# Chunk states kept by group and chunk instead of by chunk and group, in a two-layer S5 and attention network

## The chip, the core and the metric

One core of one Trainium2 chip runs the whole program. The engines are PE (the matmul engine; PEld is its weight load, which runs beside the matmuls), VectorE (DVE in the profile), ScalarE (ACT), POOL and SP, which issues the DMAs. The metric is the device time of one execution in microseconds; before the change it is 2419.13 us, the median of three runs (2417.30 to 2419.89).

## What is computed

The reference is a two-layer network for 128 prompt tokens and 512 sample tokens of 1024 features. Each layer normalizes and modulates its input, projects it, and runs three branches beside each other: a bidirectional state space scan (S5), a window attention and a global attention. They are merged with gates, projected, and followed by an MLP. What matters here is the S5 branch: 32 groups of 16 channels, 64 complex states per group and direction.

```python
def _s5_bidirectional(u, lam_re, ..., s0):
    lam_bar = jnp.exp(lam * step)
    b_bar = ((lam_bar - 1.0) / lam)[..., None] * lax.complex(b_re, b_im)
    for d, rev in ((0, False), (1, True)):
        bu = jnp.einsum('blgc,gpc->blgp', uf, b_bar[d])
        if s0 is not None:                      # the sample has an initial state
            bu = bu.at[:, n_tok - 1 if rev else 0].add(lam_bar[d] * s0c)
        _, states = lax.associative_scan(_ssm_combine, (a, bu), reverse=rev, axis=1)
        y = y + jnp.einsum('blgp,gcp->blgc', states, c_mat[d]).real
        finals.append(states[:, 0] if rev else states[:, -1])
```

The outputs are the two token arrays, the prompt's final S5 states and its keys and values.

## The kernel before

The tokens are cut into chunks of 8. There are 84 chunk columns: 16 of the prompt, 64 of the sample, and 4 of padding. The states at the chunks' starts are kept in one tile per layer, `st`, on 128 partitions (64 states of the forward direction, 64 of the backward one), and along a partition in the order [chunk, real/imaginary, group], 84 x 2 x 32 floats. It is made, changed and used in this order, once per layer:

- `s5_in` (L588), once for each four groups: 8 matmuls of 84 columns (L596), then ScalarE copies the forward half into `st` one column later (L598) and VectorE the backward half, turned round within prompt and sample (L600).
- `s5_states` (L633): POOL clears the padding, then the scan over the chunks runs in pairs of columns. `pairs(2, 3)` (L654) adds lambda^8 times each even column to the next one, in four pieces, three on VectorE and one on POOL, each of two multiplies (L660) and two adds (L661). SP copies the sample's initial state into column 19 (L664). Then come 31 dependent steps on POOL (L677 to L680), four instructions each, which carry the state two columns on; the first 8 do prompt and sample together (128 elements), the rest the sample (64 elements). `pairs(1, 2)` fills in the columns between. ScalarE takes the prompt's final state (L684), and ScalarE and VectorE turn the backward columns round again (L689 to L691).
- The outputs of the chunks (L1010 to L1026): for each group one matmul with the chunk's own inputs (L1023, moving operand `ub`) and two with the states (L1025, moving operand `st[:, :, r_, g_]`, which steps over the chunks). Each matmul of this type (float32) leaves two records in the trace.

Around this run the other branches: the key and query projections, evicted by VectorE and ScalarE (L717 to L719, L782 to L785), the window attention (L855 to L977), the low parts of the weights (L124, whose high parts come from L123) and gates worked out ahead (L813). L792 on POOL raises the queries' sums of squares to a power. The code of the two layers is the same; in layer 1 `s5_states` comes before the key projections, in layer 0 behind them. Each engine takes its instructions in one fixed order, which a scheduler has chosen with its own cost model from the program text and its dependences, so a change in one place can reorder the instructions around it on all engines.

Elsewhere, the tile `yT` is kept as [feature block, token in the chunk, chunk] and is read and written with the token in the chunk as the inner index (`y_views`, L1057), which is a step of 84 floats. Its instructions are L120 to L124 by way of `split_y` (L1062), and L1133.

Of the kernel before, what the change touches and what calls it, by code (L numbers as in the profile page):

```python
# [15 lines left out]
NT = 5                      # token tiles of 128: 0 the prompt, 1..4 the sample  # L16
D = 1024
NCH = 84                    # chunk columns: [pad, 16 prompt, pad, pad, 64 sample, pad]
# [5 lines left out]
AHEAD = ((0, 1, 4, 2, 4, 1), (1, 0, 1, 2, 4, 1))   # gates worked out ahead: beside the queries, the scan, beside its outputs, around the GLU, by layer  # L24
# [3 lines left out]
SPLITS = ((0, 3), (3, 5))   # token-tile ranges of a feature-major product  # L28


def net(tc, I, O, depth=DEPTH, dbg=None):
# [37 lines left out]
    # ---------------------------------------------------------------- constants  # L69
# [38 lines left out]
    # persistent work  # L108
# [8 lines left out]
    def split(hi, lo, src, half=False):  # L117
        """src (or src / 2) as a high part and the exact rest"""
        if half:
            S.activation(hi, src, AF.Copy, scale=0.5)  # L120
            V.scalar_tensor_tensor(lo, src, 0.5, hi, op0=ALU.mult, op1=ALU.subtract)
        else:
            S.activation(hi, src, AF.Copy)  # L123
            V.tensor_tensor(lo, src, hi, op=ALU.subtract)  # L124

    def wtile(src, K, slot=None):
        """a packed weight tile [128, 1024] of K row blocks as its high and low parts: [(hi, lo)] by row block"""
# [17 lines left out]
    def tok(a, t0, t1):  # L145
        """the token tiles t0..t1 of a view [128, NT, 128], or of the views of the two parts of SPLITS"""
# [5 lines left out]
    def mm_fm(out, ws, acts, t0, t1, ks=None, first=True, last=True):  # L152
        """feature-major: out [128 f, tokens] += w[k].T @ act[k]; ws[k] = (hi, lo) [128, 128];
        acts[k] = (hi, lo) views of the tokens"""
# [8 lines left out]
    def mm_tm(out, ws, acts, t, first=True, last=True):  # L163
        """token-major: out [128 tok, n] += act[k][:, t].T @ w[k]; ws[k] = (hi, lo) [128, n]"""
# [9 lines left out]
    # ---------------------------------------------------------------- adaLN modulation  # L174
    def mods_steps(l, rounds, tmp, tmp2=None, acc=False):
        """the modulation vectors of a layer, 2048 columns a round, one row block of the weight a step"""
        if rounds[0] == 0:
            SY.dma_start(bmodT, I["bmodT"][:, l])
        for r in rounds:
# [22 lines left out]
            # the gates as rows  # L202
# [11 lines left out]
    def affine(l, w):  # L214
        """affA/affB[l][:, w]: h = xhat * A + B; w 0: before w_in, 1: before w_up"""
# [11 lines left out]
    # ---------------------------------------------------------------- h: transposed, modulated, split  # L227
    def new_h():
        """high and low parts, each in the two parts of SPLITS"""
# [26 lines left out]
    # ---------------------------------------------------------------- layer norm of a token tile  # L256
    def ln_stat(st):
        """mean, rstd, - mean rstd from the bn_stats of the chunks"""
# [8 lines left out]
    def ln_tile(z, st):  # L267
        """z [128, 1024] -> (z - mean) * rstd in place; st: bn_stats of its chunks"""
# [4 lines left out]
    # ---------------------------------------------------------------- S5 tables (weights only)  # L273
    def s5_prep(l, pp, after=None, use=None):
# [25 lines left out]
        def poly(o, r, cs):  # L300
            """cs: from the highest power, to the constant"""
# [8 lines left out]
        def expm1(o, x, plus1=False):  # L310
            """exp(x) - 1 (or exp(x)): x = k ln2 + r"""
# [8 lines left out]
            tt(q, q, r, ALU.add)                       # e^r - 1  # L320
# [3 lines left out]
            p2 = ti.bitcast(F32)                       # 2^k  # L324
# [12 lines left out]
        # sin and cos - 1 of th: th = q 2pi + r, a = r/4, two doublings  # L337
# [19 lines left out]
        # powers of lam_bar: Pw[:, ri, k, g], k = 0..8; n = lam_bar - 1  # L357
# [27 lines left out]
        # b_bar = (lam_bar - 1) / lam * b  # L385
# [13 lines left out]
        # ec[t]: fwd lam^(t+1), bwd lam^(8-t);  ei[j]: fwd lam^(7-j), bwd lam^j  # L399
# [12 lines left out]
        for b in range(8):  # L412
# [31 lines left out]
            # C lam^e and its negated imaginary part  # L444
# [10 lines left out]
            # lag kernel of these four groups; stationary columns: [full | fwd | bwd]  # L455
# [15 lines left out]
            # input operator, built with states on partitions and transposed  # L471
# [20 lines left out]
    # ---------------------------------------------------------------- phase A  # L492
    def phase_a(l, h):
# [9 lines left out]
        if l == 0:  # L503
# [3 lines left out]
            # the rows of a partial sum over four row blocks: one from each strip  # L507
# [4 lines left out]
            # the first three row blocks of the S5 input go along  # L512
# [3 lines left out]
            def mods0(g_):  # L516
                """shift and scale of 256 features"""
# [57 lines left out]
        # entry states by chunk column, the backward direction turned round inside each segment  # L575
        st = sp.tile([128, NCH, 2, 32], F32, name="st")
# [11 lines left out]
        def s5_in(b, io):  # L588
            """what the chunks of four groups add to the states"""
# [15 lines left out]
        # ---- S5 input, to the chunked layout  # L605
# [27 lines left out]
        def s5_states():  # L633
            """the states at the chunks' starts"""
# [6 lines left out]
            # ---- scan over chunks: entry[i + 1] = lam^8 entry[i] + v, prompt and sample side by side, in pairs:  # L641
            # w = lam^8 v[i] + v[i + 1]; entry[i + 2] = lam^16 entry[i] + w one after the other; the entries between them
# [11 lines left out]
            def pairs(src, dst):  # L654
                """dst + 2 k += lam^8 (src + 2 k), all 41 pairs of columns"""
# [8 lines left out]
            SY.dma_start(st[:, 19], I["state0"][:, l])  # L664
# [17 lines left out]
            # final states of the prompt  # L682
# [691 lines left out]
    h = None  # L1374
# [3 lines left out]
    for p in (wp, ps, dram, base):  # L1378
        p.release()


# ---- host: layouts only
def pack(inp):
    import numpy as np

# [88 lines left out]
```

## Time and profile before

| what | value |
|---|---|
| median of three runs | 2419.13 us (2417.30 to 2419.89) |
| the profiled execution, first to last instruction | 2422.9 us |
| busy: PE, PEld, DVE, ACT, POOL | 2305.5, 2201.2, 1501.1, 992.3, 567.6 us |
| chain that ended last, by engine | PE 78%, DVE 8%, POOL 6%, DMA 3%, ACT 2%, issue 2% |
| mean granted clock of PE | 0.977 of full speed |
| scan of layer 0 and of layer 1 on POOL | about 216 to 282 us, and 1360 to 1430 us |

Only the span of the profiled execution is recorded for it, so it also stands for its own time; it is 3.8 us above the median of the runs. Matmuls are pipelined, so the distance between two starts tells what one costs, and the length of one contains the waiting of the pipeline. A window of the span shows which engine is full in a stage; the waits show who stood for whom; the groups by line and shape give the duration of one instruction.

### The profile page before, as it was taken

How to read it: one execution, taken by the hardware profiler on the slowest of the kernel's cores; microseconds unless marked ns; L12 is line 12 of the kernel's file. 1: busy time of each engine (PE TensorE's matmuls, PEld its weight loads, DVE VectorE, ACT ScalarE, POOL GpSimd, SP SyncE). 2: the span in 40 equal slices, each digit the busy share in tenths (PEclk: the TensorE clock that was granted, in tenths of full speed). 3: DMA queues.
4: the chain of work that ended last, by engine and by line, in shares of the span. 5: the costliest groups of instructions: out<-in, count | busy, mean ns of one | idle time of the engine just before them, and what ended most of it. 6: DMA issues, size and time to landing. Idle time of an engine off the chain costs nothing.

```text
span 2422.9 us, 43760 instructions
## 1 busy us (share of the span) xinstructions
PE 2305.5 (95%) x17304; PEld 2201.2 (91%) x17304; DVE 1501.1 (62%) x3091; ACT 992.3 (41%) x2320; POOL 567.6 (23%) x665
## 2 busy tenths in 40 slices
PE   7887999999999999999999889999999889999997
PEld 4777897799999999999999889999999889999997
DVE  6887854766357966654664766466744873444467
ACT  2324655574344333222234256467643343232221
POOL 2555700001024211100541651000102350000056
PEclk8998999999999999999999999999999999999999
DMA  7423236612241344455326223511222332222221
GB/s 261 144 82 103 97 111 225 230 68 89 72 158 54 115 164 157 162 174 200 122 97 189 72 67 111 158 61 71 77 75 72 146 100 75 76 73 79 71 73 59
DMA packets 126381, 278.25 MB, mean 115 GB/s; under 512 B 40640, under 2 KB 60224, under 8 KB 126176
## 3 DMA queue, kind: packets, MB, share of 16 engines
q1 hardware_dynamic: 126176, 275.45, 33.5%
q8 instruction: 136, 2.23, 0.4%
q14 instruction: 69, 0.57, 0.1%
HBM read 240.97 MB, written 38.63 MB: 115 GB/s over the span
## 4 chain that ended last, share of the span: by engine, by line
PE 78%; DVE 8%; POOL 6%; DMA 3%; ACT 2%; issue 2%; SPq 0%; DVEq 0%; ACTq 0%; POOLq 0%
PE p_g L159 9%; PE p_g L161 9%; PE p_g L160 9%; PE p_sc L170 4%; PE p_sc L172 4%; PE p_sc L171 4%; PE p_g L170 4%; PE p_sc L160 4%; PE p_g L171 4%; PE p_sc L161 4%; PE p_sc L159 4%; PE p_g L172 4%; PE p_pt L947 2%; PE p_g L1025 2%; POOL sa L677 1%
## 5 line engine op out<-in xcount | busy, mean ns | idle before, releaser
L124 DVE TENSOR_TENSOR wlo<-raw,whi 128x512 fp32r<-128x512 f32 x472 | 364.5, 785 | 194.4 <-ACT whi L123 188.6
L123 ACT ACTIVATE whi<-raw 128x512 fp32r<-128x512 f32 x472 | 293.5, 630 | 416.8 <-PE p_sc L172 138.8
L159 PE MATMUL p_g<-hh,whi 128*128 128x384 f32 (+1 forms) x1200 | 379.4, 316 | 2.8 <-ACT mt L802 2.6
L161 PE MATMUL p_g<-hh,wlo 128*128 128x384 f32 (+1 forms) x1200 | 377.4, 315 | 2.5 <-DVE wlo L124 2.2
L160 PE MATMUL p_g<-hl,whi 128*128 128x384 f32 (+1 forms) x1200 | 377.8, 315 | 0.0
L159 PEld LDWEIGHTS p_g<-hh,whi 128*128 128x128 f32 x1200 | 227.8, 190 | 10.1 <-ACT rl L1274 5.8
L161 PEld LDWEIGHTS p_g<-hh,wlo 128*128 128x128 f32 x1200 | 227.7, 190 | 4.3 <-DVE wlo L124 3.7
L160 PEld LDWEIGHTS p_g<-hl,whi 128*128 128x128 f32 x1200 | 228.2, 190 | 0.6 <-issue 0.5
L159 PE MATMUL p_sc<-hh,whi 128*128 128x256 f32 (+1 forms) x672 | 209.1, 312 | 9.1 <-ACT hh L123 8.8
L160 PE MATMUL p_sc<-hl,whi 128*128 128x256 f32 (+1 forms) x672 | 208.2, 310 | 4.1 <-DVE hl L124 4.1
L161 PE MATMUL p_sc<-hh,wlo 128*128 128x256 f32 (+1 forms) x672 | 208.4, 310 | 1.5 <-DVE wlo L124 1.5
L1090 POOL TENSOR_TENSOR mt<-sg,mt 128x640 f32<-128x640 f32 x24 | 41.2, 1719 | 652.1 <-DVE stat L934 272.4
L170 PE MATMUL p_sc<-whi,ff 128*128 128x256 f32 x680 | 192.9, 284 | 0.0
L172 PE MATMUL p_sc<-whi,ff 128*128 128x256 f32 x680 | 192.3, 283 | 0.0
L171 PE MATMUL p_sc<-wlo,ff 128*128 128x256 f32 x680 | 191.1, 281 | 0.0
L170 PE MATMUL p_g<-whi,hh 128*128 128x256 f32 x544 | 161.8, 299 | 10.8 <-DVE rt L785 6.6
L171 PE MATMUL p_g<-wlo,hh 128*128 128x256 f32 x544 | 161.3, 297 | 8.9 <-DVE wlo L124 8.6
L172 PE MATMUL p_g<-whi,hl 128*128 128x256 f32 x544 | 159.8, 295 | 0.0
L124 DVE TENSOR_TENSOR pl<-p_pt,ph 128x512 fp32r<-128x512 f32 (+1 forms) x176 | 102.8, 589 | 69.0 <-ACT ph L123 60.8
L159 PEld LDWEIGHTS p_sc<-hh,whi 128*128 128x128 f32 x672 | 131.0, 195 | 15.3 <-ACT hh L123 9.7
L159 PE MATMUL p_g<-act,whi 128*128 128x384 f32 x448 | 140.3, 313 | 3.7 <-ACT mtmp L192 2.3
L170 PE MATMUL p_g<-whi,ff 128*128 128x256 f32 x500 | 142.0, 284 | 0.0
(410 smaller groups left out, 6371.8 us busy)
## 6 DMA issues: line engine op xcount, KB each, us to landing
raw<-in_w_mod_dram SPq DMA_DIRECT2D x96, 512.0 KB
raw<-in_w_up_dram SPq DMA_DIRECT2D x64, 512.0 KB
raw<-in_w_down_dram SPq DMA_DIRECT2D x64, 512.0 KB
raw<-in_w_gate_dram SPq DMA_DIRECT2D x48, 512.0 KB
raw<-in_w_br_dram SPq DMA_DIRECT2D x24, 512.0 KB
raw<-in_w_q_dram SPq DMA_DIRECT2D x16, 512.0 KB
ctab_d<-prow SPq DMA_DIRECT2D x16, 512.0 KB
tab<-ctab_d SPq DMA_DIRECT2D x16, 512.0 KB
```

The lines of the kernel that those rows point to most:

```text
L123: S.activation(hi, src, AF.Copy)
L124: V.tensor_tensor(lo, src, hi, op=ALU.subtract)
L159: T.matmul(out, wh, tok(ah, t0, t1), start=(first and k == 0), stop=False)
L160: T.matmul(out, wh, tok(al, t0, t1), start=False, stop=False)
L161: T.matmul(out, wl, tok(ah, t0, t1), start=False, stop=(last and k == n - 1))
L170: T.matmul(out, ah, wh, start=(first and k == 0), stop=False)
L171: T.matmul(out, ah, wl, start=False, stop=False)
L172: T.matmul(out, al, wh, start=False, stop=(last and k == n - 1))
L677: G.tensor_tensor(a[:, 0:ns], at(cur), lb(M[:, 0]), op=ALU.mult)
L947: T.transpose(p[:, (2 * (z - z0) + z_) * 128:(2 * (z - z0) + z_ + 1) * 128], Ps[z_][:, z * 128:(z + 1) * 128], ident)
L1025: T.matmul(o, ct[:, r_, q], st[:, :, r_, g_], start=False, stop=(r_ == 1))
L1090: G.tensor_tensor(mtv[:, ft], sg, mtv[:, ft], op=ALU.add)
```

## The change

`st` becomes a view of a tile `stm` whose order along a partition is [real/imaginary, group, chunk]. All instructions of the scan keep their code, their element order and their number, and address the new tile through the view. The matmuls of the chunk outputs read the tile directly. The initial state is copied by DMA into a small tile `s0` of its own, and from there by VectorE into column 19. The final state's copy is written for the new order. The rest of the difference takes away comments.

```diff
-        # entry states by chunk column, the backward direction turned round inside each segment
-        st = sp.tile([128, NCH, 2, 32], F32, name="st")
+
+        stm = sp.tile([128, 2, 32, NCH], F32, name="st")
+        st = stm.rearrange("p r g c -> p c r g")
         segs = ((0, 18), (18, 84))
...
             pairs(2, 3)
-            SY.dma_start(st[:, 19], I["state0"][:, l])
+            s0 = sp.tile([128, 2, 32], F32, name="s0")
+            SY.dma_start(s0, I["state0"][:, l])
+            V.tensor_copy(st[:, 19], s0)
...
-            S.activation(fin, st[:, 17].rearrange("p a b -> p (a b)"), AF.Copy)
-            # the backward direction back into chunk order
+            S.activation(fin.rearrange("p (a b) -> p a b", a=2), st[:, 17], AF.Copy)
+
...
-                    T.matmul(o, ct[:, r_, q], st[:, :, r_, g_], start=False, stop=(r_ == 1))
+                    T.matmul(o, ct[:, r_, q], stm[:, r_, g_], start=False, stop=(r_ == 1))
```

In the rows of order below, the changed kernel's line numbers are one higher from L577 on and three higher from L667 on (L660 and L661 are L661 and L662 there, L684 is L687, L792 is L795).

VectorE, layer 0, the start of `pairs(2, 3)`, before the change. `VV` and `KL` belong to the attention's keys, `kf` are keys, `ub` is the product's buffer:

```order
L124 TENSOR_TENSOR VV<-vf_1506,VV 128x10x64
L660 TENSOR_TENSOR ub<-st,lam_100 128x640
L124 TENSOR_TENSOR KL<-p_pt,KH 128x512
L752 TENSOR_TENSOR kf_2012<-kf_2012,ksq 128x640
L124 TENSOR_TENSOR KL<-p_pt,KH 128x512
L661 TENSOR_TENSOR st<-st,ub 128x10x64
```

The same place in the changed kernel:

```order
L124 TENSOR_TENSOR VV<-vf_1506,VV 128x10x64
L661 TENSOR_TENSOR ub<-st,lam_100 128x640
L755 TENSOR_TENSOR kf_2012<-kf_2012,ksq 128x640
L124 TENSOR_TENSOR KL<-p_pt,KH 128x512 x2
L662 TENSOR_TENSOR st<-st,ub 128x10x64
```

The pairs keep their place, but for the order of their neighbours.

POOL, layer 0, the end of the scan, before:

```order
L678 TENSOR_TENSOR sb<-st,l_2176 128x64
L679 TENSOR_TENSOR sa<-sa,st 128x64
L680 TENSOR_TENSOR st<-sa,sb 128x64
L792 TENSOR_TENSOR ssq<-ssq,mh 128x40
L1090 TENSOR_TENSOR mt<-sg,mt 128x640 x8
```

And in the changed kernel, with three whole steps still to come:

```order
L681 TENSOR_TENSOR sb<-st,l_2176 128x64
L682 TENSOR_TENSOR sa<-sa,st 128x64
L795 TENSOR_TENSOR ssq<-ssq,mh 128x40
L683 TENSOR_TENSOR st<-sa,sb 128x64
L680 TENSOR_TENSOR sa<-st,l_2176 128x64
```

The power of the queries' sums has moved from behind the scan to between two instructions of its 28th step of 31.

ScalarE, layer 0, behind the scan, before. `fin` is the final state, the first instruction that waits for the scan's end; `whi`, `ph`, `P` and `gt` belong to weights, attention and gates:

```order
L123 ACTIVATE ph<-p_pt 128x512
L123 ACTIVATE ph<-p_pt 128x256
L684 ACTIVATE fin<-st 128x64
L689 ACTIVATE ub<-st 64x576
L938 ACTIVATE P,stat<-p_sc,stat 128x512 x2
L813 ACTIVATE gt<-p_g 128x384
L691 ACTIVATE st<-ub 64x576
```

And in the changed kernel:

```order
L941 ACTIVATE P,stat<-p_sc,stat 128x512 x2
L816 ACTIVATE gt<-p_g 128x384
L687 ACTIVATE fin<-st 128x64
L692 ACTIVATE ub<-st 64x576
L123 ACTIVATE ph<-p_pt 128x512
L694 ACTIVATE st<-ub 64x9x64
```

The first instruction that waits for the scan stands 17 instructions further back in ScalarE's order than before.

## Rows read from the trace of the kernel before

**Rows 1.** Windows: length, busy PE, PEld, DVE, ACT, POOL (us), clock, DMA.

```profile
200.00:240.00 40.00, 29.23 (x222) 27.15 (x222) 35.54 (x60) 17.36 (x74) 32.44 (x45) 0.87 0.39 118
...
240.00:300.00 60.00, 56.51 (x419) 52.95 (x417) 50.16 (x98) 38.36 (x121) 45.63 (x91) 1.00 0.28 93
...
324.00:360.00 36.00, 36.00 (x271) 34.74 (x270) 17.68 (x38) 19.18 (x49) 0.00 (x0) 1.00 0.41 141
...
1343.00:1376.00 33.00, 29.01 (x252) 27.33 (x251) 30.23 (x43) 8.87 (x18) 23.23 (x28) 1.00 0.24 81
...
1376.00:1456.00 80.00, 67.84 (x490) 64.97 (x490) 54.67 (x110) 40.00 (x146) 50.93 (x107) 0.91 0.18 60
```

**Rows 2.** Waits (total, times, longest us): 200 to 300, then 1343 to 1456.

```profile
PE p_g L170 <- DVE rt L785: 3.6, 2, 2.9
...
PE p_g L171 <- DVE wlo L124: 8.1, 8, 2.2
...
PE p_g L170 <- DVE rt L718: 3.7, 1, 3.7
...
DVE ub L660 <- POOL st L680: 11.2, 3, 7.0
```

**Rows 3.** Timeline of PE, layer 0's chunk outputs: start, length (us), instruction.

```profile
324.45 0.35 PE L1023 MATMUL p_g<-ub,mg 128*128 128x84 f32 x2
...
324.64 0.76 PE L1025 MATMUL p_g<-st,tab 128*128 128x84 f32 x4
...
325.22 0.36 PE L1023 MATMUL p_g<-ub,mg 128*128 128x84 f32 x2
```

**Rows 4.** Chain of waits, layer 1's chunk inputs: start, length (us), piece.

```profile
1317.38 2.64 PE p_sc L596 x24
```

**Rows 5.** Groups by line and shape: count, busy us, mean ns, idle before.

```profile
L124 DVE TENSOR_TENSOR wlo<-raw,whi 128x512 fp32r<-128x512 f32 x472 | 364.5, 785 | 194.4 <-ACT whi L123 188.6 <-PE p_g L160 3.9 <-PE p_pv L955 0.7
...
L1133 DVE SCALAR_TENSOR_TENSOR yT<-sg,yT 128x512 f32<-128x512 f32 x8 | 8.9, 1118 | 0.9 <-ACT sg L1131 0.9
...
L124 DVE TENSOR_TENSOR act<-yT,act 128x512 fp32r<-128x512 f32 x8 | 8.7, 1093 | 0.6 <-ACT act L123 0.6
...
L124 DVE TENSOR_TENSOR act<-yT,act 128x128 fp32r<-128x128 f32 x8 | 3.0, 380 | 0.4 <-ACT act L123 0.4
...
L690 DVE COPY st<-st 64x640 f32<-64x640 f32 x6 | 2.9, 492 | 2.1 <-ACT ub L689 2.0
...
L123 ACT ACTIVATE whi<-raw 128x512 fp32r<-128x512 f32 x472 | 293.5, 630 | 416.8 <-PE p_sc L172 138.8 <-PE p_g L160 92.7 <-DVE acc L1297 76.8
...
L123 ACT ACTIVATE act<-yT 128x512 fp32r<-128x512 f32 x8 | 9.2, 1153 | 0.0
```

**Rows 6.** The tile st: count, shortest/median/longest ns, starts, shapes.

```profile
L660 DVE TENSOR_TENSOR ub<-st,lam x24: 807/876/2189, 202.3 to 1433.6; 128x640 f32<-128x640 f32 x16, 128x704 f32<-128x704 f32 x8
...
L661 DVE TENSOR_TENSOR st<-st,ub x24: 806/888/2190, 207.1 to 1435.6; 128x640 f32<-128x640 f32 x16, 128x704 f32<-128x704 f32 x8
...
L598 ACT ACTIVATE st<-p_sc x32: 435/440/442, 91.4 to 1342.3; 64x332 f32<-64x332 f32 x32
```

**Rows 7.** Timelines of POOL and of DVE, layer 1, the start of the pairs.

```profile
1343.51 2.22 POOL L660 TENSOR_TENSOR ub<-st,lam 128x640 f32<-128x640 f32 x1 [0.21 <-DVE st L600]
...
1344.33 1.94 DVE L124 TENSOR_TENSOR wlo<-raw,whi 128x512 fp32r<-128x512 f32 x1
```

**Rows 8.** POOL: a group by shape, and a wait from 200 to 300.

```profile
L792 POOL TENSOR_TENSOR ssq<-ssq,mh 128x40 f32<-128x40 f32 x2 | 13.8, 6919 | 49.9 <-DVE ssq L790 49.9
...
POOL sa L677 <- DMA st<-in_state_dram: 5.9, 1, 5.9
```

**Rows 9.** ACT timeline, last turned columns; chain, first outputs of layer 1.

```profile
297.87 0.36 ACT L691 ACTIVATE st<-ub 64x192 f32<-64x192 f32 x1
...
1451.53 0.36 ACT L691 ACTIVATE st<-ub 64x192 f32<-64x192 f32 x1
...
1490.98 0.60 PE p_g L1025 x4
```

## The prediction

> **What bounds the kernel now.** I read first the stages around the chunk scan (busy time by window), then the tensor engine's timeline where the chunk outputs stand, then the waits inside the scan, and last the rows that show what a stride of 84 floats costs. The program is bound by PE as a whole; the changed tile `st` is touched in two places per layer, and they have different limits.
>
> The first place is the scan. In layer 0 (200 to 300 us) VectorE is nearly full: 35.5 of 40 us, then 50.2 of 60 us, and PE loses time there, 10.8 and 3.5 us [rows 1]. In layer 1 (1343 to 1456) VectorE has 30.2 of 33, then 54.7 of 80 us, and PE loses 4.0 and 12.2 us [rows 1]. What PE waits for there is VectorE: an eviction at L785 (3.6 us in layer 0), the low weight parts of L124 (8.1 us) and an eviction at L718 (3.7 us) in layer 1; VectorE in turn stands 11.2 us at L660 behind a POOL scan step [rows 2]. VectorE takes its instructions in order, so whatever lengthens an instruction on `st` lengthens what is queued behind it, the evictions included.
>
> The second place is the chunk outputs at L1025. From 324 to 360 us PE is busy 36.00 of 36 us [rows 1], so there a cheaper matmul is a shorter program.
>
> **The matmul that gets a dense operand.** L1025 reads its moving operand, 84 columns, with a step of 64 floats now; L1023 beside it, of the same shape and type, reads 84 adjacent columns. By their starts, the two at 324.45 take 0.095 us each, the four at 324.64 take 0.145 us each [rows 3]. The dense 84-column matmuls of L596 run 24 in 2.64 us, 0.110 us each [rows 4]. There are 256 L1025 records. The gain is 256 x 0.035 = 9.0 us by L596, or 256 x 0.050 = 12.8 us by L1023. I take 11 us, between the two, since L596 starts new sums and L1023 is the direct neighbour.
>
> **What the vector instructions on `st` pay.** Element order stays [chunk, re/im, group], so the inner step becomes 84 floats where it was 1. No instruction of the kernel before has this on `st`, but the tile `yT` is read and written with just this step. VectorE: 128 elements 380 ns, 512 elements 1093 ns, that is 1.86 ns per element; with the output strided as well, 512 take 1118 ns [rows 5]. Continued to 640 elements this is 1331 ns for a strided input and 1356 ns for strided input and output; to 704, 1450 and 1475 ns. L660 and L661 now take 807 and 806 ns at their shortest (the 640 form); I take 0.89 us for 704 by their share of elements [rows 6]. So each rises by 0.52 to 0.59 us. One call of pairs() has 12 on VectorE (8 of 640, 4 of 704): 4 x 0.52 + 4 x 0.55 + 2 x 0.56 + 2 x 0.59 = 6.6 us. Two calls a layer, two layers: 26.3 us. The copies of L690 run at 492 ns for 640 elements [rows 5]; at 1.86 ns plus the 0.14 us left over at 128 elements they would take 1.33 us. Three of 640 and two smaller ones a layer give about 3.3 us, 6.5 us in all, the other bound being nothing. Together VectorE gets 32.8 us more.
>
> How much reaches PE? Lower bound: it fills VectorE's idle time in its own window, and only the overflow counts: 6.6 - 4.5 and 6.6 - 2.8 for the first calls, 9.9 - 9.8 and 0 for the rest, 6 us. Upper bound: all, 32.8 us. The first call stands where VectorE is 89 to 92% busy and PE waits right behind it, so I count it in full, 13.2 us. The second call and the turning round stand where PE itself is nearly full in layer 0 and VectorE has 25 us idle in layer 1, and the order now has them up to 17 places later; I count a quarter of 19.8, 5 us. That is 18 us.
>
> Sharing makes this worse rather than better: while POOL runs a 128x640 instruction of 2.22 us, an L124 of VectorE takes 1.94 us [rows 7], against 0.79 us in the mean over all 472 of them [rows 5]. The Trainium skill, page "SBUF — State Buffer", section "Who interferes with whom", says that a VectorE instruction with two SBUF inputs contends with a GpSimd instruction that reads SBUF; the two rows agree. By it, each POOL instruction that gets longer would hold a VectorE one for the difference, and the sum would be up to 10 us higher (16 pair instructions x 0.65 us); I leave it in the range.
>
> **ScalarE.** L689, L691 and L684 get the step too. A strided read costs 1153 against 630 ns for 512 elements, 1.02 ns more per element [rows 5]; 2688 elements a layer, read, and perhaps the same again written: 2.7 to 5.5 us a layer. L598 only writes `st` (440 ns for 332 elements [rows 6]); a strided write alone has no row, so 0 to 0.34 us each, 32 times, in stages where ScalarE is far from full. These copies stand among the exponentials of the window attention, but beside a full PE. I take 2 us out of 0 to 10.
>
> **The scan on POOL.** No POOL instruction of the kernel before reads with a long step. Bounds: nothing, or ScalarE's 1.02 ns per strided element. Three of the four instructions of a step read `st`, 2496 elements a layer: 0 to 7.6 us; the eight POOL pair instructions 0 to 5.2 us. In layer 0 the order also puts the 6.9 us power of L792 [rows 8] into the 28th of the 31 steps instead of behind the last. Against that, the initial state is there early, where POOL stood 5.9 us until its transfer had landed [rows 8]; the new 64-element copy is some 0.2 us of VectorE. What hides the rest is slack: the last turned columns are written at 298.2 us and L1025 begins at 324.6 in layer 0 [rows 3, 9]; 1451.9 against 1491.0 in layer 1 [rows 9]. At the upper bound layer 0 ends 12.8 + 6.9 + about 9 (last pairs and turning) = 29 us later, less up to 5.9, against a slack of 26.4: just covered. What is left is VectorE and ScalarE standing behind a later scan step, and the order has moved their instructions back for that. I take 2 us.
>
> **Sum.** -11 + 18 + 2 + 2 = +11 us. The profiled execution has a span of 2422.9 us, 3.8 us above the median of the three runs, 2419.13; 2422.9 + 11 = 2433.9 in its own terms, 2430 on the median (+0.45%). A measurement of this kernel can tell about 0.2%, 4.8 us, from no change.
>
> **Rivals.**
> 1. *The vector time is free, and only the matmul counts.* VectorE has 42 us idle in the four windows [rows 1], more than the 32.8 us added, and the instructions of the second call stand further back. If PE's waits grow by less than 11 us the kernel is faster. With nothing lost: 2419 - 11 = 2408 us; with the 6 us overflow, 2414. Against it: VectorE's idle time lies mostly in 1376 to 1456, and the first calls have only 7 us of it. Chance 0.22.
> 2. *Both cancel*: PE's loss comes out at 7 to 15 us, within 4.8 us of the gain. Chance 0.20, 2419 us.
> 3. *The scan takes the place of the wait.* If POOL pays 2 ns per strided element, its part in layer 0 grows by 15.3 + 10.4 + 6.9 = 33 us, and with 9 us of turning passes the 26.4 us of slack by 15; L1025 then waits for `st`. In layer 1 26 + 9 stays under 39 us, but the 11.2 and 3.7 us waits [rows 2] grow, some 8 us. 2430 + 23 = 2453 us. It decides from about 1 ns per element. A rule for it: the Trainium skill, page "Advanced Engine Details and Errata", section "Memory Cachelines", says that SBUF has 16-byte lines and that an access to a different line each time is penalized, whichever engine reads. Rows 3 and 5 agree for PE, VectorE and ScalarE; no row shows POOL. By it the change makes one reader dense and all the others sparse. Chance 0.13.
> 4. *The step isn't what makes L1025 slow* (it also adds to a running sum, which L596 does not): no gain, 2441 us. Against it: L1023 opens the same sum and has the same weights' size. Chance 0.07.
>
> **How the numbers follow.** The forecast itself, a loss of PE time at the scan that is larger than the gain at L1025, has 0.38, with its own range from 2425 to 2440 us. Faster 0.22, same 0.20, slower 0.38 + 0.13 + 0.07 = 0.58. The range for 8 in 10 reaches from 2408 (rival 1 with no loss) to 2455 (rival 3, or the upper bound of 32.8 with rows 7's contention).
>
> **What would show it.** Right: L1025's four take 0.38 to 0.44 us instead of 0.58; L660 and L661 on VectorE have their shortest at 1.3 to 1.45 us; PE's busy share in the four windows falls, with waits for L124, L718 and L785. Wrong: L660 and L661 stay near 0.8 us, or they double and the scan stage is no longer than 100 us in layer 0; L1025 stays at 0.145 us; PE's loader waits at L1025 for a ScalarE or VectorE write of `st`, which would be rival 3.

## The result, and the profile after

The changed kernel takes 2453.94 us (median of four runs, 2450.86 to 2457.08), the kernel before 2419.51 us beside it. The ratio is 1.0142, with a 95% interval of 1.0127 to 1.0156: 34 us slower, where 11 us slower was forecast. The profiled execution has a span of 2453.4 us. Below, a difference of two ratios is turned into us with 2419.5; an interval of 0.001 to 0.0024 either way is 2.5 to 6 us, and a difference of two such kernels is uncertain by some 4 to 7 us.

What the step costs each engine is read from the tile `st` in the changed kernel (count, shortest/median/longest ns; line numbers are those of the changed kernel, one higher from L577 and three higher from L667):

```profile
L1028 PE MATMUL p_g<-st,tab x256: 234/275/275, 341.4 to 1582.6; 128*128 128x84 f32 x128
L601 DVE COPY st<-p_sc x64: 267/443/637, 94.6 to 1356.2; 64x68 f32<-64x68 f32 x32, 64x260 f32<-64x260 f32 x32
L680 POOL TENSOR_TENSOR sa<-st,l x62: 346/410/1721, 220.9 to 1457.9; 128x64 f32<-128x64 f32 x46, 128x128 f32<-128x128 f32 x16
L681 POOL TENSOR_TENSOR sb<-st,l x62: 337/357/1787, 222.5 to 1458.2; 128x64 f32<-128x64 f32 x46, 128x128 f32<-128x128 f32 x16
...
L599 ACT ACTIVATE st<-p_sc x32: 722/739/778, 91.7 to 1355.2; 64x332 f32<-64x332 f32 x32
L661 DVE TENSOR_TENSOR ub<-st,lam x24: 1468/1502/3069, 200.0 to 1468.6; 128x640 f32<-128x640 f32 x16, 128x704 f32<-128x704 f32 x8
L662 DVE TENSOR_TENSOR st<-st,ub x24: 1475/1630/2993, 206.7 to 1471.5; 128x640 f32<-128x640 f32 x16, 128x704 f32<-128x704 f32 x8
L692 ACT ACTIVATE ub<-st x10: 595/1500/1532, 306.3 to 1485.4; 64x640 f32<-64x640 f32 x6, 64x576 f32<-64x576 f32 x2, 64x192 f32<-64x192 f32 x2
L693 DVE COPY st<-st x10: 420/826/834, 307.8 to 1486.2; 64x640 f32<-64x640 f32 x6, 64x576 f32<-64x576 f32 x2, 64x192 f32<-64x192 f32 x2
L694 ACT ACTIVATE st<-ub x10: 598/1522/1533, 308.6 to 1490.5; 64x640 f32<-64x640 f32 x6, 64x576 f32<-64x576 f32 x2, 64x192 f32<-64x192 f32 x2
L661 POOL TENSOR_TENSOR ub<-st,lam x8: 1877/2123/3114, 199.3 to 1415.7; 128x640 f32<-128x640 f32 x8
...
L687 ACT ACTIVATE fin<-st x2: 335/335/335, 306.0 to 1459.3; 128x64 f32<-128x64 f32 x2
```

VectorE's pairs went from 807 and 806 ns at their shortest [rows 6] to 1468 and 1475. L599, which only writes `st`, went from 440 to 739 ns [rows 6]; no row of the kernel before had shown such a write. The turning round on ScalarE doubled. A single step of POOL's scan hardly moved at its shortest (L681, 316 to 337 ns), but the scan did: in layer 0 it now runs from 220.9 us to 306.0, where `fin` stops waiting, 85 us instead of 66. All VectorE work on `st` sums to 112.06 us, against 70.56 before.

The gain is there too. The timeline of PE at layer 0's chunk outputs answers [rows 3]; the four L1028 now take 0.45 us from start to start (341.40 to 341.85), where they took 0.58. Behind them stands the row of ScalarE that answers [rows 9], the last turned columns of layer 0; they are written at 329.8 us instead of 298.2:

```profile
341.22 0.34 PE L1026 MATMUL p_g<-ub,mg 128*128 128x84 f32 x2
341.40 0.61 PE L1028 MATMUL p_g<-st,tab 128*128 128x84 f32 x4
341.85 0.39 PE L1026 MATMUL p_g<-ub,mg 128*128 128x84 f32 x2
...
329.24 0.60 ACT L694 ACTIVATE st<-ub 64x192 f32<-64x192 f32 x1
```

Where the time went is seen in windows of the changed kernel (length, busy PE, PEld, DVE, ACT, POOL, then PE's granted clock and DMA). The first three are those of [rows 1]; the two of layer 1 are stretches of its own, since everything there comes later:

```profile
200.00:240.00 40.00, 23.33 (x150) 21.38 (x149) 37.85 (x51) 12.28 (x55) 28.08 (x27) 0.74 0.28 90
240.00:300.00 60.00, 54.15 (x390) 50.96 (x389) 49.39 (x90) 32.50 (x118) 56.71 (x94) 0.94 0.25 82
324.00:360.00 36.00, 33.28 (x243) 30.73 (x243) 21.07 (x42) 25.27 (x56) 0.00 (x0) 1.00 0.36 120
1356.00:1400.00 44.00, 34.45 (x249) 32.63 (x248) 41.10 (x46) 9.03 (x19) 34.72 (x33) 0.81 0.18 60
1456.00:1500.00 44.00, 34.67 (x230) 31.69 (x229) 32.07 (x62) 33.43 (x96) 2.93 (x9) 0.81 0.18 58
```

At 200 to 240 us PE got through 150 records instead of 222, VectorE was nearly full, and the granted clock of PE fell from 0.87 to 0.74 of full speed. At 324 to 360, where PE had been full, it now has idle time; the chunk outputs begin there 17 us later (341.4 against 324.6). What PE waits for is mostly VectorE, in the waits of 197 to 315 us and then of 1356 to 1490 us (total, times, longest):

```profile
PE p_pt L871 <- DVE KL L124: 7.5, 1, 7.5
PE p_g L170 <- DVE rt L788: 4.7, 2, 3.8
PE p_pv L958 <- DVE pl L124: 4.1, 4, 1.4
...
PE p_g L171 <- DVE wlo L124: 10.3, 4, 4.3
PE p_g L170 <- DVE rt L721: 5.2, 2, 3.2
PE p_sc L918 <- ACT P L941: 3.9, 2, 3.2
PE p_pt L950 <- DVE qs L876: 2.8, 1, 2.8
```

None of these waits is for `st`. They are for low weight parts, evictions, keys and queries that stand behind the longer instructions in the order of VectorE, and in one row for ScalarE's exponentials `P`.

### The profile page after: what moved, and what is told of

Same layout as the page of the kernel before. It is cut to its first block, busy times and chain, and to the rows that moved or that the text cites. A ratio compares the mean times of both kernels' runs of the same rounds, so it can differ in the third digit from the quotient of the medians.

```text
span 2453.4 us, 43747 instructions
## 1 busy us (share of the span) xinstructions
PE 2309.2 (94%) x17304; PEld 2203.1 (90%) x17304; DVE 1548.2 (63%) x3093; ACT 1016.8 (41%) x2320; POOL 599.2 (24%) x665
## 5 line engine op out<-in xcount | busy, mean ns | idle before, releaser
L124 DVE TENSOR_TENSOR wlo<-raw,whi 128x512 fp32r<-128x512 f32 x472 | 370.9, 799 | 194.0 <-ACT whi L123 187.9
L1278 DVE TENSOR_TENSOR rl<-rl 128x384 f32<-128x384 f32 (+1 forms) x128 | 75.6, 592 | 107.8 <-ACT rl L1277 107.7
```

The lines of the kernel that those rows point to most:

```text
L1278: V.tensor_tensor(r[:, :n], r[:, :n], r[:, :n], op=ALU.mult)
```

## The experiments

**Which users of `st` cost the time.** Three kernels keep the new layout and the dense matmul, and change the loops so that the chunk is the inner index: then a pair instruction has an inner step of 2 floats, and the copies one of 1. One kernel leaves the layout as it was and reads another, dense operand.

`e1_all_inner`: copies in, pairs and turning round by chunk; only POOL's scan, the final state and the copy of the initial state keep the long step.

```diff
-                S.activation(st[0:64, 1:NCH, r_, 4 * b:4 * b + 4], v[0:64, 0:NCH - 1], AF.Copy)
+                S.activation(stm[0:64, r_, 4 * b:4 * b + 4, 1:NCH], v[0:64, :, 0:NCH - 1], AF.Copy)
...
-                    x_, o = (st[:, c + 2 * k:c + 2 * (k + n) - 1:2] for c in (src, dst))
+                    x_, o = (stm[:, :, :, c + 2 * k:c + 2 * (k + n) - 1:2] for c in (src, dst))
...
-                x0, x1 = st[64:128, a:a + n], st[64:128, e - n:e]
+                x0, x1 = stm[64:128, :, :, a:a + n], stm[64:128, :, :, e - n:e]
```

> The changed layout, but all instructions on the states apart from the scan's own steps, the new state's copy and the final state's copy run with the chunk as the inner index (steps of 1 or 2 floats): pairs, the copies into the tile, the turning round, the first clearing. Only the scan on POOL, 64 elements at a time, keeps the step of 84 floats. My theory (VectorE's pairs and copies at the long step hold up the evictions): the 34 us are gone and the matmuls' gain stays, about 2411 us, 0.3% below the kernel before. Rival A (POOL's strided scan steps cause it): still above 2435 us. Rival B (the new order of the instructions causes it, whatever they cost): anywhere, but L660 and L661 at 0.8 us while the kernel stays above 2430 us.

`e2_pairs_inner`: of this only the pairs (the second piece of the diff).

> The changed kernel with the pairs alone run with the chunk as the inner index (step 2 floats); the copies into the tile and the turning round keep the step of 84. My theory: VectorE's pairs are the largest part, 26 us of VectorE time in two layers, so about 2428 us. Rival (the copies and ScalarE's share of them are the largest part): 2445 us or more.

`e3_rest_inner`: all of it but the pairs.

> The changed kernel with everything but the pairs turned: the copies into the tile, the turning round and the first clearing run with the chunk as the inner index, the pairs keep the step of 84 floats. My theory: about 8 us come back, 2446 us. Rival (ScalarE and VectorE copies are the largest part): 2425 us or less.

`e4_out_dense`: the kernel before, with a dense operand in L1025, the chunk's own inputs. It leaves the states' part out of the outputs and prices the matmul alone.

```diff
-                    T.matmul(o, ct[:, r_, q], st[:, :, r_, g_], start=False, stop=(r_ == 1))
+                    T.matmul(o, ct[:, r_, q], ub[:, (b % 2) * 4 + q], start=False, stop=(r_ == 1))
```

> The kernel before; the two matmuls per group that read the states read the chunk's own inputs in their place (84 adjacent columns), so the states' part of the outputs is left out. It prices the gain alone. My theory: 256 matmul records at 0.095 to 0.110 us instead of 0.145 us, 9 to 13 us less, about 2409 us. Rival (the step is not what makes them slow, but the sum they add to): 2419 us. Rival (the gain is lost behind the outputs' transfers): 2415 us or more although the records are shorter.

| kernel | median, us | ratio to before (95%) | against the change, us |
|---|---|---|---|
| the change | 2453.94 | 1.0142 (1.0127 to 1.0156) | |
| e1, all by chunk | 2407.05 | 0.9952 (0.9937 to 0.9967) | -46.0 |
| e2, pairs by chunk | 2420.23 | 1.0013 (1.0003 to 1.0024) | -31.2 |
| e3, all but the pairs | 2436.29 | 1.0076 (1.0060 to 1.0092) | -16.0 |
| e4, before, dense operand | 2408.25 | 0.9965 (0.9953 to 0.9976) | |

The pairs are 31 us and the rest is 16, which makes 47; both in one kernel are 46, so within the intervals they add up. Both are more than the theory expected (about 26 and 8), the rest twice as much. The matmul's gain alone is 8.5 us (0.35%), give or take 3. With the long step gone from everything but POOL's scan, the new layout is faster than the kernel before by 11.6 us: this is the version that beats both. Its tile `st` shows that VectorE's pairs pay nothing for a step of 2 floats, and that ScalarE's copies, whose elements are adjacent again, take what they took before (same columns as above):

```profile
L599 ACT ACTIVATE st<-p_sc x32: 440/440/442, 91.5 to 1330.8; 64x332 f32<-64x332 f32 x32
L661 DVE TENSOR_TENSOR ub<-st,lam x24: 808/881/2009, 198.5 to 1428.8; 128x640 f32<-128x640 f32 x16, 128x704 f32<-128x704 f32 x8
...
L692 ACT ACTIVATE ub<-st x10: 345/725/747, 291.1 to 1437.9; 64x640 f32<-64x640 f32 x6, 64x576 f32<-64x576 f32 x2, 64x192 f32<-64x192 f32 x2
...
L661 POOL TENSOR_TENSOR ub<-st,lam x8: 1292/1505/2033, 197.8 to 1380.3; 128x640 f32<-128x640 f32 x8
```

**The small tile alone.** `e5_s0_only`: the kernel before, in which the initial state goes through `s0`.

```diff
-            SY.dma_start(st[:, 19], I["state0"][:, l])
+            s0 = sp.tile([128, 2, 32], F32, name="s0")
+            SY.dma_start(s0, I["state0"][:, l])
+            V.tensor_copy(st[:, 19], s0)
```

> The kernel before, with one part of the change alone: the initial state goes by DMA into the small tile s0 and from there by VectorE into column 19; the layout of the states stays. Theory: the small tile is worth nothing to the time, because what it frees (POOL stands 5.9 us for the transfer in layer 0 and has 26 us of slack) is not on the path: 0.998 to 1.002 of before, 2414 to 2423 us. Rival: the earlier start of the scan is part of why the all-dense variant beat the change by 46 us and the kernel before by 12: then this one is at 2407 to 2413 us.

2412.24 us, ratio 0.9981 (0.9970 to 0.9991): 4.6 us faster. By its median it is inside the rival's range, by its ratio still inside the theory's (the kernel before took 2417.02 us beside it); that there is a gain at all is clear of the interval. But it isn't the earlier start of the scan that the rival supposed: in layer 0 POOL now waits 8.2 us for the copy, which stands in VectorE's order, where it waited 5.9 us for the transfer [rows 8].

```profile
POOL sa L679 <- DVE st L666: 8.2, 1, 8.2
```

The order of the instructions differs from that of before on PE already ahead of the scan, by the scheduler's choice, and in the two profiled executions the 900th matmul starts 6.9 us earlier, at 146.8 us instead of 153.7, where the scan has not begun. The change and all its variants have the small tile and are early there too (146.6 to 150.5 us); e4, which has not, is at 154.1. So part of what the change moved was other work, ahead of the scan. The gain of e4 and this one add up to 13.1 us, e1's is 11.6; so POOL's longer scan steps cost 1.5 us by these medians. The three intervals together leave 5 us either way, and e1's order of instructions is not e5's, so the 1.5 us are not resolved.

**Which pairs.** `e6_pairs_vector`: the change, with VectorE's pieces by chunk and POOL's as in the change. `e7_pairs_first`: with the first call by chunk. `e10_pairs_second`: with the second. The edit is the pairs' line of e1 under a condition, `if e is V`, `if src == 2` or `if src == 1`.

> The changed kernel with VectorE's three pieces of each pairs() call running with the chunk as the inner index (a step of 2 floats); POOL's piece keeps the inner step of 84 floats, and so do all copies. All pieces dense gave 31 us of the changed kernel's 34. Theory: it is VectorE's own time (24 instructions 0.6 us longer), so nearly all of the 31 us comes back here: 2421 to 2427 us, VectorE's L661 and L662 at 0.8 us for 640 elements. Rival: it is the longer pieces of POOL, which hold VectorE through the memory they share and delay the scan: then 10 us or less come back, 2442 us or more, and VectorE's instructions beside POOL's pieces stay above 1.2 us.

> The changed kernel with only the first call, pairs(2, 3), running with the chunk as the inner index; the second call and all copies keep the inner step of 84 floats. It tests the weights of the prediction, which counted the first call in full and the second to a quarter. By those weights four fifths of the pairs' 31 us come back: about 2427 us. Rival A: both calls weigh alike, because VectorE has no real idle time behind the scan either: half comes back, about 2437 us. Rival B: the second call weighs more, because it stands behind POOL's scan and in front of the turning round: a third or less comes back, 2442 us or more.

> The changed kernel with only the second call, pairs(1, 2), running with the chunk as the inner index. All pairs dense gave 31 us, the first call alone 23. Theory: the two calls add up, so 6 to 10 us come back: about 2444 us. Rival: the gains overlap, because the second call waits for a scan that the first one delays: then 12 us or more come back (2440 us or less), or 4 or less (2448 us or more).

| kernel | median, us | ratio to before (95%) | against the change, us |
|---|---|---|---|
| e6, VectorE's pieces | 2426.96 | 1.0043 (1.0029 to 1.0056) | -24.0 |
| e7, first call | 2428.64 | 1.0046 (1.0032 to 1.0060) | -23.2 |
| e10, second call | 2443.27 | 1.0109 (1.0085 to 1.0133) | -8.0 |

First and second call make 31.2 us, all pairs in one kernel 31.2: they add up, with some 7 us of uncertainty from e10. Three quarters of the pairs' cost belong to the call in front of the scan, close to the four fifths of the prediction's weights, and three quarters to VectorE's pieces. The other 7 us, between e6 and e2, came with POOL's longer pieces and with an order of instructions that changes with them.

The first call cost 23 us. It made VectorE's work on `st` 17.0 us longer (95.08 to 112.06 us from e7 to the change) and POOL's pieces 5.1 us (32.0 to 37.1). The same ten microseconds of layer 0 in the change and then in e7 (columns as in the windows above) show how that becomes more:

```profile
214.00:224.00 10.00, 2.90 (x10) 2.15 (x10) 9.83 (x12) 4.33 (x19) 2.97 (x4) 0.50 0.00 0
```

```profile
214.00:224.00 10.00, 7.22 (x48) 7.20 (x48) 9.91 (x19) 3.65 (x19) 9.53 (x13) 0.68 0.04 13
```

VectorE is full in both, with 12 and 19 instructions. In the change PE mostly stands, as it did in the ten microseconds before (2.51 us busy, granted 0.92), and it is granted 0.50 of full speed throughout, the lower of its two levels, 1.2 of 2.4 GHz; in e7 it does 48 records at 0.68. The waits there, in the timeline of PE in the change (start, length, instruction, idle before):

```profile
215.71 1.12 PE L871 MATMUL p_pt<-ident,qw 128*128 128x128 f32 x4 [7.46 <-DVE KL L124]
218.41 0.48 PE L918 MATMUL p_sc<-KH,qs 128*128 128x128 f32 x1 [1.59 <-DVE qs L875]
224.16 0.58 PE L170 MATMUL p_g<-whi,hh 128*128 128x256 f32 x1 [3.85 <-DVE rt L788]
```

e6 allows a closer look. On PE, VectorE, ScalarE and POOL it runs the same operations on the same tiles in exactly the order of the change, so the same matmul can be timed in both traces, one execution each. Over the first call the change's PE falls behind e6's by 8.1 us in layer 0 (a lag of 1.6 us at 201 us of e6, of 9.7 at 238) and by 8.2 in layer 1 (16.9 at 1349, 25.1 at 1396); over the second call by 3.8 (10.2 at 246, 14.0 at 324) and 4.0 (25.0 at 1417, 29.0 at 1471). VectorE's pieces are 15.1 us longer in the two first calls (28.0 to 43.1 us) and 16.3 in the two second ones (21.3 to 37.6). So with the order unchanged, VectorE's added time cost PE about its own length in the first calls and half of it in the second. What e7 finds beyond these 16 us, some 7, came with POOL's pieces and another order; no run parts the two.

The order of e3 is that of the change as well, e2 and e8 have that of e1, and e4 has that of the kernel before; e7, e9 and e10 have orders of their own. So the scheduler's order did not react to the steps of VectorE's and ScalarE's instructions (e3 and e6 against the change, e8 against e1), and it did to POOL's (e2 against e6).

**Is it VectorE's time or the step?** `e9_more_dense`: e1, in which each VectorE piece of the first call does its first multiply three times and its second twice.

```diff
-                    for xv, lv in ((x_, L0), (x_[:, ::-1], L1)):
+                    for xv, lv, m in ((x_, L0, 3), (x_[:, ::-1], L1, 2)):
+                        for _ in range(m if e is V and src == 2 else 1):
```

> The dense variant (2407 us) with more VectorE work in the first call of pairs() and no long step anywhere: of each VectorE piece the first multiply is done three times and the second twice, into the same buffer, so nine dense instructions of about 0.83 us a layer are added, 15 us in all. That is what the step of 84 floats added to VectorE in the first call (its busy time fell by 14.6 us, from 1548.2 to 1533.6, when that call alone was made dense, and the time by 23 us). Theory: the loss is VectorE's queue and nothing about the step itself; the time rises by 15 us or more, since TensorE's granted clock falls as well where it waits: 2422 to 2432 us. Rival A: the long step disturbs the other engines' accesses to the memory, and that made 15 us into 23: then dense work costs clearly less than its own length, below 2419 us. Rival B: the scheduler sees this work, which it did not see of the step, and moves other work between it; then the time is also below 2419 us, but the order of VectorE there shows other instructions between the pairs than in the dense variant.

2415.37 us, ratio 0.9982 (0.9973 to 0.9991): VectorE's work on `st` rose by 17.1 us over e1 (69.58 to 86.71), as much as the first call's step had added, its whole busy time by 12.2 (1505.1 to 1517.3), and the time by 7.3. That is an outcome which both rivals named, and the order decides for rival B, at least in part. The timeline of VectorE in e9 from the first multiply on, then one row of e1, and then the first multiply and the same eviction in the change:

```profile
196.19 2.01 DVE L662 TENSOR_TENSOR ub<-st,lam 128x640 f32<-128x640 f32 x1
...
206.79 0.82 DVE L663 TENSOR_TENSOR st<-st,ub 128x640 f32<-128x640 f32 x1
...
209.57 0.68 DVE L876 SCALAR_TENSOR_TENSOR qs<-p_pt,qs 64x512 fp32r<-64x512 f32 x1
...
211.01 1.58 DVE L662 TENSOR_TENSOR ub<-st,lam 128x640 f32<-128x640 f32 x2
...
214.34 0.42 DVE L789 TENSOR_TENSOR rt<-p_g,qn 128x256 f32<-128x256 f32 x1
...
216.65 0.91 DVE L663 TENSOR_TENSOR st<-st,ub 128x640 f32<-128x640 f32 x1
```

```profile
216.79 0.42 DVE L788 TENSOR_TENSOR rt<-p_g,qn 128x256 f32<-128x256 f32 x1
```

```profile
199.98 3.07 DVE L661 TENSOR_TENSOR ub<-st,lam 128x640 f32<-128x640 f32 x1
...
223.69 0.42 DVE L788 TENSOR_TENSOR rt<-p_g,qn 128x256 f32<-128x256 f32 x1
```

Up to the eviction of the queries (L789, L788 in e1) VectorE has done one add of the pairs in e9, but three in e1 (at 203.90, 209.08 and 214.21); with the multiplies it is seven instructions of the pairs in both. The eviction comes 18.2 us behind the first multiply in e9 and 18.3 in e1 (198.47): the time that the added work takes was put behind it. In the change it comes 23.7 us behind.

So work that stood in the program as instructions went behind what PE waits for, and cost 7.3 us, give or take 4, for 17.1 us of VectorE; the step's added time stood ahead of it, in nearly the order of the dense variant, and cost 23.2 us, give or take 5, for 17.0 of VectorE and 5.1 of POOL's pieces. Whether the step also disturbs the other engines' accesses this run can't tell, since it changed two things.

**The turning round.** `e8_turn_long`: e1, in which only the turning round keeps the step of 84 floats.

```diff
-                x0, x1 = stm[64:128, :, :, a:a + n], stm[64:128, :, :, e - n:e]
+                x0, x1 = st[64:128, a:a + n], st[64:128, e - n:e]
```

> The dense variant (2407 us: copies in, pairs and turning round with the chunk as the inner index) in which only the turning round behind the second call keeps the inner step of 84 floats. Pairs alone dense gave 2420 us, so copies in and turning round together are worth 13 us there. Theory: the turning round carries 10 us or more of it, since it stands behind the scan, where the pairs-dense variant lost 7 us of TensorE time in layer 0 and 5 us in layer 1: 2416 to 2421 us. Rival: the copies in carry it, ScalarE's 0.3 us for each of 32 and VectorE's 0.2 us for each of 64, in the stage where the states are made: 2407 to 2411 us here.

2416.83 us, ratio 0.9996 (0.9984 to 1.0008): 10.6 us above e1, as the theory had it; the copies in are left with 4.1 us (e2 against e8). In this kernel ScalarE works 12.6 us longer on `st` than in e1 (40.35 against 27.77 us) and VectorE 3.1 us. The two kernels run in one order, and PE in e8 falls behind e1's by 5.9 us between 289 and 317 us of e1 and by 4.8 between 1418 and 1456. The windows of 286 to 330 us of e1 and then of e8, and behind them two rows of ScalarE and two of PE in e8, show how it reaches PE:

```profile
286.00:330.00 44.00, 42.41 (x311) 39.56 (x310) 30.01 (x58) 31.54 (x69) 4.33 (x13) 1.00 0.33 104
```

```profile
286.00:330.00 44.00, 37.54 (x266) 33.82 (x265) 28.66 (x51) 33.88 (x60) 1.70 (x6) 1.00 0.29 92
...
291.16 1.40 ACT L694 ACTIVATE st<-ub 64x576 f32<-64x576 f32 x1 [0.93 <-DVE st L693]
292.58 0.60 ACT L123 ACTIVATE ph<-p_pt 128x512 fp32r<-128x512 f32 x1
...
293.23 0.39 PE L957 MATMUL p_pv<-ph,VV 128*128 128x256 f32 x1 [1.34 <-ACT ph L123]
...
308.65 0.36 PE L957 MATMUL p_pv<-ph,VV 128*128 128x256 f32 x1 [2.48 <-DVE qw L966]
```

ScalarE has 10 us to spare in that stretch and PE loses 4.9 us all the same: the high part `ph` of the attention's weights stands behind L694 in ScalarE's order, and PE waits 1.34 us for it. The longest wait, 2.48 us, names VectorE's L966; it stands behind two copies of the turning round in VectorE's order (L693 at 304.90 and 306.49 us), of which the first had waited 0.86 us for ScalarE's L692.

## Why the prediction came out as it did

The direction and the mechanism were right: a gain at the outputs, and a larger loss at the scan, because longer instructions of VectorE delay what is queued behind them. The size was not: 34 us instead of 11. The measured time lies at the upper end of the prediction's range, and it is the 2453 us of rival 3, whose wait did not come about; that this number fits is luck. Term by term:

| term | forecast, us | measured, us | from |
|---|---|---|---|
| dense operand | -11 (9.0 to 12.8) | -8.5 | e4 |
| first call of the pairs | +13.2 | +23.2 | e7 |
| second call | +3.3, a quarter of 13.2 | +8.0, give or take 7 | e10 |
| turning round, VectorE and ScalarE | +1.6, and part of ScalarE's 2 | +10.6 | e8 against e1 |
| copies in | part of ScalarE's 2; L600 not counted | +4.1 | e2 against e8 |
| POOL's scan | +2 | about +1.5, not resolved | e1 less e4 and e5 |
| small tile and the order around it | nothing | -4.6 | e5 |
| sum | +11 | +34 | |

The rows of the table come from differences of neighbouring variants, so that they sum to the whole is no test of its own; that the two calls measured apart make the pairs measured together is one, as far as the intervals reach.

- **The gain** was sized by two rows, and the lower, [rows 4], was right: 256 x 0.033 us by e4, and 0.45 us for four in the trace, where 0.38 to 0.44 were named as the sign. The dense L1026 beside them still takes only 0.09 us by its starts, so the operand was not all that set L1023 apart.
- **The duration of a strided instruction** was nearly right. 1.33 us was continued from 512 to 640 elements of `yT`; the shortest is 1.47, and the mean of the 640 form went from 1019 to 1681 ns, 0.66 us more instead of 0.52 to 0.55. VectorE's whole work on `st` grew by 41.5 us, not 32.8. Summed one by one the pairs grew by 33.0 us instead of 26.3, the copies of L690 by 2.3 instead of 6.5, and those of L600, which the prediction did not price at all, by 7.7 (6.1 of it the 260 form, 13.6 to 19.7 us).
- **"How much reaches PE?" is the step that failed.** It counted the first call at its length, 13.2 us, and a quarter, 5 us, of the second call and the turning round, because VectorE has idle time where they stand, with 2 us for ScalarE. Measured are 23.2 us for the first call and 8.0 + 10.6 + 4.1 = 22.7 us for the rest. Idle time in a window of 80 us is no cover for an instruction that stands in front of one which PE needs next: with the order unchanged, half of the second calls' added VectorE time reached PE (e6), and the turning round cost 10.6 us for 3.1 us of VectorE and 12.6 of ScalarE. For VectorE's part of the first calls the length was the right measure (16.3 us of PE for 15.1 of VectorE), but POOL's pieces, which the sum set at next to nothing, and the order that changes with them came with some 7 us more. Where VectorE held PE up, PE's clock fell too: [rows 1] had 0.87 at 200 to 240 us, the change 0.74.
- **ScalarE** was taken at 2 out of 0 to 10, because its copies stand beside a full PE. In e8 PE is no longer full in that stretch. That L598 would pay for a strided write was left open between 0 and 0.34 us; it pays 0.30.
- **POOL's scan** was set at 2 us; the 1.5 us of e1 agree, unresolved. But its length was not foreseen. Alone a step pays little: the shortest on `st` (L678, now L681) went from 316 to 337 ns for 64 elements, 0.3 ns per element, below the 1 ns from which rival 3 decides. Beside VectorE's pairs a step lasts longer: by the traces, the steps of 64 elements that run mostly beside one take 0.84 us in the mean before and 1.22 in the change, those beside no VectorE instruction 0.32 and 0.35. All steps together went from 117.9 to 141.2 us, 23 us more, where the prediction's upper bound was 7.6 a layer; e6, with the same long step on POOL and short ones on VectorE, has 126.1, so 15 us of this come with VectorE's longer pairs. Rival 3 still did not come about: in layer 0 the last turned columns are written at 329.8 us and L1028 begins at 341.4, so 11.6 us of the 26.4 of slack are left, and no wait of PE is for `st`. The rule that the prediction weighed there, from the Trainium skill, page "Advanced Engine Details and Errata", section "Memory Cachelines", speaks of lines of 16 bytes and of two hits on a line. It agrees with e1 and the change on VectorE, where a step of 2 floats costs nothing (808 against 807 ns) and one of 84 costs 660 ns; on POOL it shows in the pairs (1292 ns with 2 floats, 1877 with 84) and hardly in the scan's shortest steps.
- **Rivals 1 and 2** fell by the same rows: VectorE's 42 us of idle time did not cover the change. Rival 4 fell with e4, where the operand alone gave 8.5 us.
- **The small tile** was priced at its 0.2 us of copy and at most 5.9 us of earlier start; it gave 4.6 us, by another order of the work around it. Part of it is there before the scan begins; what in that order gives it wasn't followed further.

What stays open is how the some 7 us that the first call cost beyond VectorE's part divide between POOL's pieces, the other order, and accesses that disturb each other; and how much of all these costs is PE's lower clock, which is seen, but which no run held fixed.

## What to carry to other kernels

A layout is read and written by several engines, so price the change for each of them, the plain copies included, and look for a loop order that gives every one of them a short step: here the same layout with the chunk as the inner index turned 34 us of loss into 12 us of gain. What added time on an in-order engine costs can't be read from that engine's idle time in the window: here the same instructions cost PE their whole length in one place and half of it in another. Look at the instruction that stands right behind, and who waits for that. Where a scheduler has set the order, a cost to which it does not react can weigh more than one that it can place: here 23.2 against 7.3 us for the same time of VectorE.

## What the runs showed of the hardware

- ScalarE pays for a strided write alone as it does for a strided read: 332 elements from 440 to 739 ns (0.90 ns per element), and 640 read with the step from 736 to 1532 ns (1.24, the longest of each).
- VectorE's copy of 640 elements with the step on both sides is dearer by only 0.33 us (826 against 492 ns), while the multiply and the add of the pairs rise by 0.66 us, nearly twice that, for the same number of elements.
- POOL's 640-element multiply took 1542 ns at its shortest with adjacent elements and 1292 ns with a step of 2 floats and the other operand constant along the inner index: the dense layout was not its fastest form. Its add did not gain (1560 and 1587 ns).
- POOL's small instructions take longer beside longer VectorE ones. With one order of instructions and the same long step on POOL, the longest of L681's scan steps (L690 in e6) takes 1181 ns in e6, where VectorE's pairs take 809 ns at their shortest, and 1787 ns in the change, where they take 1468; the shortest is 339 and 337 ns.
